# A stick-breaking and retention step: values and gates of one head as one 512-column row panel, in place of two-head value panels and gate panels

## The chip, the cores and the metric

The kernel runs on one core of a Trainium2 chip. The metric is the device time of one execution in microseconds. The kernel before takes 2279.3 us, the median of three runs (2276.02 to 2281.19).

A core has TensorE for matmuls (PE in the profile; its loads of the stationary operand are PEld), VectorE (DVE), ScalarE (ACT), GpSimd (POOL) and SyncE (SP), which here only issues transfers. Each engine works through its own list of instructions in order, and semaphores tie the lists together. ACT, POOL and SP each issue DMAs from their own list, so a transfer also waits for what stands ahead of it there.

## The reference

One layer of a hybrid encoder, for 1024 prompt frames and 8 x 16 sample frames (one tile of 128), with a model width of 2048 and 8 heads of 128 in each of two groups. One projection gives eight parts; stick-breaking attention and retention work on four each; each head's output is normalised and multiplied by the SiLU of its gate; then comes one output projection.

```python
p = jnp.einsum('btd,de->bte', rms_norm(x, norm_pre), w_in)
q_sb, k_sb, v_sb, gate_sb, q_r, k_r, v_r, gate_r = jnp.split(p, splits, axis=-1)
# stick-breaking
z = jnp.einsum('bqhd,bkhd->bhqk', q, k) * (HEAD_DIM ** -0.5)
later = lax.cumsum(log_keep, axis=3, reverse=True) - log_keep
a = jnp.where(strict, jnp.exp(log_beta + later), 0.0)
o_sb = jnp.einsum('bhqk,bkhd->bqhd', a, v)
# retention, by chunks, with a state s
o_r = intra(q, k) @ v + decay_read * (q @ s)
# merge
y = concat(head_rms_norm(o_sb, g_sb) * silu(gate_sb), head_rms_norm(o_r, g_r) * silu(gate_r))
x = x + rms_norm(y @ w_out, norm_post)
```

## The kernel before

**Tiles and groups.** The frames are nine tiles of 128. Group g0 is tiles 0 to 3 and the sample tile, 640 columns in pieces of 256 and 384; group g1 is tiles 4 to 7, 512 columns in one piece. Stage 2 goes through g0 and then g1, and in each through the eight heads.

**Products.** Every large product is split in three: a number is taken as a rounded part (hi) and a rest (lo), and hi x hi, hi x lo and lo x hi are summed. `split` (L167, L168) makes both parts: ACT copies the rounded part (wh), DVE subtracts it (wl). So each weight block of 256 KB needs a load (wr, on SP's queue, five buffers), an ACT pass and a DVE pass (four buffers) before PE can use it.

**Panels.** A column panel (`project`, L401; matmul L387) keeps the weights stationary and moves the tokens of a group: 16 blocks of 128 rows, three terms each. A head has six: retention's queries and keys (parts 4, 5) and gate (7), attention's queries and keys (0, 1) and gate (3). A row panel (`project_rows`, L424; matmul L446) keeps a tile of tokens stationary and moves 256 weight columns, the values of two heads; so one is computed for each part and each pair of heads. `gate` (L475) multiplies a gate panel by the root of the norm, takes its sigmoid on ACT and multiplies both.

**Order.** The side work of the heads (scores, scans, transposes, decode, retention) is written as jobs that yield a number of ticks. `tick` (L228) adds one to a clock and lets at most one job take a step; a panel ticks as it emits its products, 48 times for a column panel. Constants such as D_TO, D_TI (from a turn-out to its turn-in and on to its transpose) and D_VC (between the two sets of decode's value products) are counted in these ticks. `drain(job)` ticks until a job has ended, whether products are emitted or not. The scheduler then sets each engine's list by this order and its priorities.

**Side work that the change touches or moves.** `decode` (L796) computes the sample tile's scores against cached keys (zc, L822), then `pd` from cached values: eight loads vc (L849) into a ring of V_BUFS = 6 buffers that the cached keys kcT also use, in two sets of four (L886). `sample_retention` updates the samples' states (pSs, pa, L1011; ro). `Out.finish` (L705) normalises a head's output, sends it to DRAM (s_o, turn-out on ACT's queue), fetches it turned (so, ro, turn-in on SP's queue), transposes it (L716) and multiplies it by gain and gate. `stick_breaking` (L727) runs z (L753), sigmoids, scan (L682), product (L683), turn-out and turn-in (be), transpose (L743) and pa (L783). `retention` has rs (L913) and pa (L931).

**PSUM.** The tags acc0 and acc1 have two banks each. z has two more (score_tile).

**End of stage 2 and stage 3.** The output projection is computed as seven products (n = 1 to 7) of blocks; product(5) for g0 runs at the end of stage 2, then the remaining jobs are drained. Stage 3 (matmuls L1210, L1213, L1214; tokens stationary, 512 weight columns moving) starts with product 1 for both groups.

Of the kernel before, what the change touches and what calls it, by code (L numbers as in the profile page):

```python
# [18 lines left out]
P = 128  # L19
# [13 lines left out]
COLS = (0, 1, 3, 4, 5, 7)  # L33
ROWS = (2, 6)
# [54 lines left out]
def tile_hybrid_step(  # L89
# [138 lines left out]
    def tick():  # L228
        clock[0] += 1
        for job in jobs:  # L230
            if job.at <= clock[0]:
                wait = step(job)
                jobs.remove(job)
                if wait is None:
                    job.done = True
                else:
                    job.at = clock[0] + wait
                    jobs.append(job)
                return
# [184 lines left out]
    def project_rows(g, mov, col, dst, off, loads=None, roots_first=None):  # L424
        hi, lo = mov
        nt = len(g["tiles"])
        banks = [
            accp.tile([P, 2, 2 * P], F32, name=f"accn{b}", tag=f"acc{b % 2}") for b in range((nt + 1) // 2)
        ]
        for w in range(KT // 2):  # L430
            wr = wp.tile([P, 2, 2 * P], F32, name="wrn", tag="wr", bufs=5)
            nc.sync.dma_start(wr, w_rows[ROWS.index(col[0]), col[1] // 2, :, 2 * w : 2 * (w + 1), :])
            for _ in range(WQ // 2 if loads and w < 2 else 0):
                next(loads, None)
            wh = wp.tile([P, 2, 2 * P], F32R, name="whn", tag="wh")
            wl = wp.tile([P, 2, 2 * P], F32R, name="wln", tag="wl")
            split(wh, wl, wr)
            for j in range(2):
                q, jj = divmod(2 * w + j, WQ)
                for t in range(nt):  # L440
                    a = banks[t // 2][:, t % 2, :]
                    ts = slice(t * P, (t + 1) * P)
                    for n, (lhs, rhs) in enumerate(((hi, wh), (hi, wl), (lo, wh))):


                        anchor[0] = nc.tensor.matmul(  # L446
                            a,
                            lhs[q][:, jj, ts],
                            rhs[:, j, :],
                            start=(w == 0 and j == 0 and n == 0 and t % 2 == 0),  # L450
                            stop=(w == KT // 2 - 1 and j == 1 and n == 2 and (t % 2 == 1 or t == nt - 1)),
                        )
                    tick()
        if roots_first:
            roots_first()
        for t in range(nt):
            at = tiles_before(g) + t
            nc.scalar.activation(
                dst[:, off + t].rearrange("p j d -> p (j d)"), banks[t // 2][:, t % 2, :], AF.Copy,
                scale=root_of[:, at : at + 1],  # L460
            )

    with ExitStack() as s1:
# [11 lines left out]
        def gate(acc, tag):  # L475
            e = ep.tile([P, NMAX], F32, name=tag, tag=tag)
            for a, (o, m) in acc:
                rooted(e[:, o : o + m], a, o, m)
                s = ep.tile([P, 512], F32, name="sw", tag="sw", bufs=1)
                nc.scalar.activation(s[:, :m], e[:, o : o + m], AF.Sigmoid)  # L480
                nc.vector.tensor_tensor(e[:, o : o + m], e[:, o : o + m], s[:, :m], ALU.mult)
            return e
# [14 lines left out]
        pair = {}  # L497

        def ret_values(g, mov, h, loads=None, roots_first=None):
            pair["r"] = ep.tile([P, 5, 2, P], F32, name="rv", tag="rv")  # L500
            project_rows(g, mov, col(6, h), pair["r"], 0, loads, roots_first)

# [8 lines left out]
        with tc.tile_pool(name="p0", bufs=2) as p0, tc.tile_pool(name="p0s", bufs=1) as p0s, tc.tile_pool(  # L511
            name="p0p", bufs=4, space=PSUM
# [92 lines left out]
            ret_values(g0, mov, 0, None, roots_first)  # L605
# [3 lines left out]
            first = *first, pair["r"][:, :, 0, :], dict(rg=gate(project(g0, mov, col(7, 0)), "rg"))  # L609
# [15 lines left out]
        def store_rows(tiles, n, off, dst_p, dst_s, h):  # L625
            nc.scalar.dma_start(dst_p[h, :, tiles[0] : tiles[0] + 4, :], n[:, off : off + 4, :])
            if SAMPLE in tiles:
                nc.scalar.dma_start(dst_s[h], n[:, off + 4, :])

        par = const.tile([P, 2, 4, 2, DS], F32, name="par")  # L630
        nc.vector.memset(par, 0.0)
        for j in range(2):
            nc.vector.memset(par[:, j, :, j, :], 1.0)
        parf = par.rearrange("p a c j t -> p a (c j t)")
# [60 lines left out]
        class Out:  # L695
# [5 lines left out]
            def done(self, i):  # L701
                sq = op.tile([P, P], F32, name="sq", tag="sq")
                nc.scalar.activation(sq, self.o[:, i, :], AF.Square, accum_out=self.ssq[:, i : i + 1])

            def finish(self, b, h, gT, oT, dst):  # L705
                rs = inv_rms(op, self.ssq, P, "o")
                nc.vector.tensor_tensor(
                    self.o, self.o, rs.unsqueeze(2).to_broadcast([P, self.nt, P]), ALU.mult
                )
                s = turn_out(self.o, f"s_o{b}_{h}_{self.nt}_{phase[0]}")  # L710
# [6 lines left out]
                nc.vector.scalar_tensor_tensor(  # L717
                    gT[:, :n], oT[:, :n], gains[:, b, h : h + 1], gT[:, :n], ALU.mult, ALU.mult
                )
                nc.scalar.dma_start(dst, gT[:, : self.nt * P])  # L720
# [6 lines left out]
        def stick_breaking(g, h, out, q2, k2, rest):  # L727
            todo = [(i, t) for i, t in enumerate(g["tiles"]) if t != SAMPLE]
            lag, kinds = 2, ("psr" if todo[0][1] else ("kp", "be", "cp"))
            rows = []  # L730
            for step in range(len(todo) + lag):
# [39 lines left out]
                if step >= lag:  # L771
# [6 lines left out]
                    while "vn" not in rest:  # L778
                        yield 3
                    vn = rest["vn"]  # L780
                    po = acc_tile()
                    for j in range(t + 1):
                        nc.tensor.matmul(po[:, :P], at[:, j, :], vn[:, j, :], start=(j == 0), stop=(j == t))  # L783
# [12 lines left out]
        def decode(h, qs, rest):  # L796
            i = 4
            out = Out(1, "do")
            qp = op.tile([P, 2, P], F32, name="qp", tag="qp", bufs=1)
            nc.vector.tensor_tensor(  # L800
                qp, qs.unsqueeze(1).to_broadcast([P, 2, P]), parf, ALU.mult
            )
# [71 lines left out]
            while "vn" not in rest:  # L874
                yield 3
            vn = rest["vn"]
            po = psd.tile([P, 512], F32, name="pd", tag="pd")
            nc.tensor.matmul(po[:, 2 * P : 3 * P], at[:, 8, :], vn[:, i, :], start=True, stop=True)
# [21 lines left out]
            while "sg" not in rest:  # L900
                yield 3
            last_row = slice(4 * P, 5 * P)
            oT = op.tile([P, P], F32, name="doT", tag="doT", bufs=1)
            Job(out.finish(0, h, rest["sg"][:, last_row], oT, s_y[0][h][:, last_row]))
# [117 lines left out]
        def ret_branch(gi, g, h, rq, rk, rv, rest):  # L1022
# [15 lines left out]
            while "rg" not in rest:  # L1038
                yield 3
            yield from out.finish(1, h, rest["rg"], rk, s_y[gi][H + h])  # L1040

        def sb_branch(gi, g, h, out, q2, k2, kT, rest):
# [9 lines left out]
            store_rows(tiles, rest["vn"], off, v_prompt, v_sample, h)  # L1052
            if gi == 0:
                nc.scalar.dma_start(s_v[h], rest["vn"][:, :4, :])
            while "sg" not in rest:
                yield 3
            yield from out.finish(0, h, rest["sg"][:, :NB_TOK], kT, s_y[gi][h][:, :NB_TOK])
# [17 lines left out]
        ret_job = sb_job = sub = loads = after = None  # L1075
# [504 lines left out]
```

## Time and profile before

| what | us |
|---|---|
| median of three runs | 2279.3 |
| profiled execution, span | 2278.3 |
| column panels, matmul L387, all pieces and terms, busy | 1989.9 |
| row panels, matmul L446, busy | 979.6 |
| split of 128x512 weight blocks on ACT (L167), mean of one | 0.631 |
| split of 128x512 weight blocks on DVE (L168), mean of one | 0.689 |
| load of a weight block wr from issue to landing, median | 4.4 |
| turn-out s_o<-so, and turn-in so<-s_o, median | 4.2, 3.0 |

A matmul's busy time in the groups overlaps that of its neighbours (the two sums above are longer than the span), so the pitch of matmuls is read from unbroken runs in the chain, not from the mean of one. In a row of the chain the columns are start, length and what ran, with the number of instructions joined. In the waits, a row names an engine and line, what it waited for, the total, the number of times and the longest. In the groups, a row gives line, engine, operation, tiles and shapes, count, then busy time and mean nanoseconds of one, then idle time ahead of it and its cause.

### The profile page before, as it was taken

To read this page: it belongs to the slowest core of one execution; us is meant where nothing else is said; L and a number is where in the kernel's file an instruction comes from. 1 tells how busy PE (TensorE), PEld (TensorE's weight loads), DVE (VectorE), ACT (ScalarE), POOL (GpSimd) and SP (SyncE) were. 2 spreads that over 40 slices of the span, in tenths; PEclk is the share of its full clock that TensorE was granted. 3 is DMA by queue.
4 is the path that set the end of the run, shared out by engine and by line. 5 is a ranking of instruction groups with operands and counts; after the bars stand their busy time and mean duration, and the time that the engine had idled before them with its cause. 6 is when DMAs were issued, how large, how long until landed. Compare 5 with 4: busy or idle time off the path is not lost.

```text
span 2278.3 us, 38962 instructions
## 1 busy us (share of the span) xinstructions
PE 2241.5 (98%) x14306; PEld 2023.3 (89%) x14306; DVE 1263.7 (55%) x2606; ACT 919.8 (40%) x1951; POOL 340.6 (15%) x577
## 2 busy tenths in 40 slices
PE   8999999999999999999999999999999999999998
PEld 8999999999999999999887989888888988788886
DVE  5435544454545454456556665766665667555567
ACT  6433333333333333335343334343343445435363
POOL 0012120301202030121111111120212212000020
PEclk9999999999999999999999999999999999999999
DMA  8747656675656657578778888878787758865596
GB/s 284 233 153 199 196 159 194 176 220 159 182 194 181 194 165 209 177 200 269 193 225 207 220 220 235 206 226 238 220 231 213 216 165 190 252 205 182 146 222 172
DMA packets 440832, 463.13 MB, mean 203 GB/s; under 512 B 182336, under 2 KB 302144, under 8 KB 440128
## 3 DMA queue, kind: packets, MB, share of 16 engines
q1 hardware_dynamic: 318400, 300.16, 46.5%
q0 software_dynamic: 28720, 78.41, 12.3%
q10 hardware_dynamic: 93520, 82.07, 11.4%
q8 instruction: 112, 1.84, 0.3%
q14 instruction: 80, 0.66, 0.1%
HBM read 359.58 MB, written 110.36 MB: 206 GB/s over the span
## 4 chain that ended last, share of the span: by engine, by line
PE 88%; DMA 5%; DVE 3%; issue 2%; ACT 2%; SPq 0%; POOL 0%; DVEq 0%; ACTq 0%; POOLq 0%
PE acc L387 46%; PE accn L446 17%; PE a L1213 5%; PE a L1214 5%; PE a L1210 5%; PE pa L783 3%; PE z L753 2%; PE pd L886 1%; PE zc L822 1%; DMA ro<-s_rk 1%; DMA s_rk<-rk 1%; PE pa L931 1%; PE pS L946 1%; DVE kp L682 1%; DMA wr<-w_cols 1%
## 5 line engine op out<-in xcount | busy, mean ns | idle before, releaser
L387 PE MATMUL acc<-mh,wh 128*128 128x256 f32 (+2 forms) x2304 | 667.4, 341 | 6.9 <-ACT wh L167 6.9
L387 PE MATMUL acc<-ml,wh 128*128 128x256 f32 (+2 forms) x2304 | 662.7, 340 | 0.2
L387 PE MATMUL acc<-mh,wl 128*128 128x256 f32 (+2 forms) x2304 | 659.8, 338 | 0.0
L168 DVE TENSOR_TENSOR wl<-wr,wh 128x512 fp32r<-128x512 f32 x504 | 345.9, 689 | 428.0 <-ACT wh L167 401.7
L167 ACT ACTIVATE wh<-wr 128x512 fp32r<-128x512 f32 x504 | 317.3, 631 | 641.2 <-PE acc L387 347.2
L387 PEld LDWEIGHTS acc<-mh,wh 128*128 128x128 f32 x2304 | 421.4, 189 | 39.2 <-ACT wh L167 6.9
L387 PEld LDWEIGHTS acc<-ml,wh 128*128 128x128 f32 x2304 | 422.9, 189 | 32.1 <-issue 3.3
L387 PEld LDWEIGHTS acc<-mh,wl 128*128 128x128 f32 x2304 | 425.5, 189 | 27.8 <-DVE wl L168 0.2
L446 PE MATMUL accn<-whn,mh 128*128 128x256 f32 x1152 | 328.1, 285 | 0.0
L446 PE MATMUL accn<-wln,mh 128*128 128x256 f32 x1152 | 325.8, 283 | 0.8 <-DVE wln L168 0.8
L446 PE MATMUL accn<-whn,ml 128*128 128x256 f32 x1152 | 325.7, 283 | 0.0
L446 PEld LDWEIGHTS accn<-whn,mh 128*128 128x128 f32 x1152 | 220.7, 192 | 2.7 <-issue 0.8
L446 PEld LDWEIGHTS accn<-wln,mh 128*128 128x128 f32 x1152 | 220.7, 192 | 1.8 <-DVE wln L168 1.0
L446 PEld LDWEIGHTS accn<-whn,ml 128*128 128x128 f32 x1152 | 220.7, 192 | 0.0
L167 ACT ACTIVATE whn<-wrn 128x512 fp32r<-128x512 f32 x128 | 80.5, 632 | 183.2 <-PE acc L387 74.2
L168 DVE TENSOR_TENSOR wln<-wrn,whn 128x512 fp32r<-128x512 f32 x128 | 87.6, 687 | 117.4 <-ACT whn L167 113.5
L646 POOL DMA_DIRECT2D be<-s_be x128 | 94.1, 741 | 149.5 <-DMA s_be<-be 126.4
L682 DVE TENSOR_TENSOR_SCAN kp<-kp 128x1152 f32<-128x1152 f32 (+4 forms) x40 | 82.7, 2067 | 45.7 <-POOL kp L671 29.1
L809 POOL DMA_DIRECT2D kcT<-cache_k x64 | 34.6, 545 | 442.2 <-PE pd L886 268.2
L1210 PE MATMUL a<-wh,mh 128*128 128x512 f32 x240 | 94.0, 392 | 1.8 <-ACT wh L167 1.8
L671 POOL TENSOR_SCALAR_AFFINE_SELECT kb<-kb 128x128 f32<-128x128 f32 x64 | 29.8, 474 | 433.2 <-ACT kb L665 430.9
L1213 PE MATMUL a<-wl,mh 128*128 128x512 f32 x240 | 94.3, 393 | 0.2 <-DVE wl L168 0.2
(272 smaller groups left out, 2968.7 us busy)
## 6 DMA issues: line engine op xcount, KB each, us to landing
wr<-w_cols SPq DMA_DIRECT2D x384, 256.0 KB, 4.4
wrn<-w_rows SPq DMA_DIRECT2D x128, 256.0 KB, 3.7
kcT<-cache_k POOLq DMA_DIRECT2D x64, 512.0 KB, 8.2
vc<-cache_v SPq DMA_DIRECT2D x64, 512.0 KB, 6.0
wr<-s_b SPq DMA_DIRECT2D x80, 256.0 KB, 4.1
br<-w_out SPq DMA_DIRECT2D x64, 256.0 KB, 4.9
s_b<-br ACTq DMA_DIRECT2D x32, 512.0 KB, 5.5
wr<-w_out SPq DMA_DIRECT2D x48, 256.0 KB, 3.7
```

The costliest lines, as they stand in the source:

```text
L167: nc.scalar.activation(hi, src, AF.Copy),
L168: nc.vector.tensor_tensor(lo, src, hi.bitcast(F32), ALU.subtract),
L387: last = nc.tensor.matmul(a[:, :m], lhs[:, j, :], rhs[w][:, j, o : o + m], start=(w == 0 and j == 0 and n == 0), stop=(w == KT // WQ - 1 a ...
L446: anchor[0] = nc.tensor.matmul(a, lhs[q][:, jj, ts], rhs[:, j, :], start=(w == 0 and j == 0 and n == 0 and t % 2 == 0), stop=(w == KT // 2 ...
L646: q.dma_start(raw[32 * i : 32 * i + 32, :].rearrange("p (k a) -> p k a", a=32), s[:, :, 32 * i : 32 * i + 32].rearrange("k (j b) a -> b (k ...
L682: nc.vector.tensor_tensor_scan(rev, rev, rev, 1.0, ALU.mult, ALU.bypass)
L753: nc.tensor.matmul(z[:, :c], q2[a][:, i * P : (i + 1) * P], k2[b][:, s : s + c], start=(m == 0), stop=(m == 2),)
L783: nc.tensor.matmul(po[:, :P], at[:, j, :], vn[:, j, :], start=(j == 0), stop=(j == t))
L809: ready.append((kc, nc.gpsimd.dma_start(kc, cache_k[h, m // 4, m % 4])))
L1210: ins = nc.tensor.matmul(a, hi[k][:, ts], wh, start=first, stop=False)
L1213: nc.tensor.matmul(a, hi[k][:, ts], wl, start=False, stop=False)
L1214: anchor[0] = nc.tensor.matmul(a, lo[k][:, ts], wh, start=False, stop=last)
```

## The change

The values and gates of one head become one row panel of 512 columns (v_sb, v_ret, g_sb, g_ret). The two gate panels of a head and the row panels of two heads go. The panel of five tiles needs five PSUM banks: four are acc0 and acc1 twice, the fifth in g0 is a z bank (in head 0 one of another pool). Each tile's bank is read by ACT (copy of 256 columns, sigmoid of 256) and DVE (256). The gate is then in rows and not in columns, so `finish` multiplies by it ahead of the turn-out, and only the gain comes after the transpose.

```diff
-    def project_rows(g, mov, col, dst, off, loads=None, roots_first=None):
+    def project_rows(g, mov, part, extra, out, loads=None, ready=None):
...
+        banks = [accp.tile([P, 512], F32, name=f"accm{t}", tag=f"acc{t % 2}") for t in range(4)]
+        if nt > 4:
+            banks.append(extra())
+        for k in range(KT):
...
+            for t in range(nt):
+                ts = slice(t * P, (t + 1) * P)
+                for n, (lhs, rhs) in enumerate(((hi, wh), (hi, wl), (lo, wh))):
+                    anchor[0] = nc.tensor.matmul(
+                        banks[t],
...
+                    if n:
+                        tick(0.75)
...
+            def out(t, a, root):
+                vt, ut = (x[:, t].rearrange("p j d -> p (j d)") for x in (v, u))
+                nc.scalar.activation(vt, a[:, : 2 * P], AF.Copy, scale=root)
+                nc.scalar.activation(ut, a[:, 2 * P :], AF.Sigmoid, scale=root)
+                nc.vector.scalar_tensor_tensor(ut, a[:, 2 * P :], root, ut, ALU.mult, ALU.mult)
+
+            project_rows(g, mov, w_rows[h], extra or (lambda: score_tile("accm4")), out, loads, ready)
...
-                nc.vector.tensor_tensor(
-                    self.o, self.o, rs.unsqueeze(2).to_broadcast([P, self.nt, P]), ALU.mult
-                )
+                for i in range(self.nt):
+                    nc.vector.scalar_tensor_tensor(
+                        self.o[:, i, :], self.o[:, i, :], rs[:, i : i + 1], gated[gi, h][:, at + i, b, :], ALU.mult, ALU.mult
+                    )
...
+                nc.vector.tensor_scalar(flat, oT[:, :n], gains[:, b, h : h + 1], None, ALU.mult)
```

The order of a head's panels changes, and with it where the jobs fall. The last head of g1 computes retention's queries and keys as one pair, with the loads of the first output products between. Product 1 for g0 moves into stage 2, ahead of the drains, and stage 3 begins with product 1 for g1 alone; the weights of n = 1 are loaded and split for each.

```diff
+                def ret_both():
+                    rest = first_left()
+                    accs = project_pair(g, mov, (col(4, h), col(5, h)), rest)
+                    for _ in rest:
+                        pass
+                    ret_finish(accs[0])
+                    ret_keys(accs[1])
+
+                def ret_finish(acc):
                     drain(ret_job)
                     rows_in["rq"] = rope(acc, "rq", *ropes)
...
-                    order = ret_queries, ret_keys, ret_gate, attention, gates
-                elif h == H - 3:
-                    order = ret_queries, ret_keys, attention, ret_gate, gates
+                    order = rows, ret_queries, ret_keys, attention
                 elif h == H - 2:
-                    order = ret_queries, attention, ret_keys, ret_gate, gates
+                    order = rows, ret_queries, attention, ret_keys
                 else:
-                    order = attention, ret_queries, ret_keys, ret_gate, gates
+                    order = rows, attention, ret_both
...
         drain(nxt)
+        for nh in range(2):
+            Job(collect(1, nh, product(1, nh, (0,), True, D_OUT)), 1)
         drain(ret_job)
         drain(sb_job)
...
-        for n, groups in ((1, BOTH), (2, BOTH), (5, G1), (3, BOTH), (6, BOTH), (7, BOTH)):
+        for n, groups in ((1, G1), (2, BOTH), (5, G1), (3, BOTH), (6, BOTH), (7, BOTH)):
```

The pacing constants keep their values. Smaller edits: the sample queries' mask is replaced by two copies into a tile that is zeroed once, and the values of g0's frames are loaded into a tile of their own for g1.

**The first place: decode's values on PE, in g0.** Before, in the head whose decode is pd_5472, the second set of four cached-value products stands 74 rows of PE behind the first, with products of the panel on both sides (vc is a cached-value block, acc0 and acc1 the panel's banks):

```order
L886 MATMUL pd_5472<-vc_5339,kp_4329 32x256 x4
L886 MATMUL pd_5472<-vc_5389,kp_4329 32x256 x4
L886 MATMUL pd_5472<-vc_5516,kp_4329 32x256 x4
L886 MATMUL pd_5472<-vc_5518,kp_4329 32x256 x4
L387 MATMUL acc0_5621<-ml1_179,wh_5659 128x256
L387 MATMUL acc1_5622<-ml1_179,wh_5659 128x384
```

Now, in the same head (pd_4798), both sets stand together, and right behind them the first product with a new weight block:

```order
L859 MATMUL pd_4798<-vv_2704,kp_3846 128x128
L867 MATMUL pd_4798<-vc_4606,kp_3846 32x256 x4
L867 MATMUL pd_4798<-vc_4608,kp_3846 32x256 x4
L867 MATMUL pd_4798<-vc_4714,kp_3846 32x256 x4
L867 MATMUL pd_4798<-vc_4730,kp_3846 32x256 x4
L867 MATMUL pd_4798<-vc_4741,kp_3846 32x256 x4
L867 MATMUL pd_4798<-vc_4747,kp_3846 32x256 x4
L867 MATMUL pd_4798<-vc_4844,kp_3846 32x256 x4
L867 MATMUL pd_4798<-vc_4846,kp_3846 32x256 x4
L386 MATMUL acc0_4958<-mh3_182,wh_5096 128x256
L386 MATMUL acc1_4959<-mh3_182,wh_5096 128x384
```

vc_4844 and vc_4846 use the buffers of vc_4606 and vc_4608, so their loads stand behind the first two of these rows; the products that lay between the sets have moved elsewhere.

**The second place: ACT behind the same decode.** Before, the decode's output do_4325 is squared, its root taken behind a table load, and then the split of a later block, wh_5888, follows; the turn-out s_o comes after it:

```order
L167 ACTIVATE wh_5826<-wr_5824 128x512
L703 ACTIVATE sq_5702,ssq2_4326<-do_4325 128x128
L183 ACT_TABLE_LOAD
L183 ACTIVATE or_5708<-ov_5707 128x1
L167 ACTIVATE wh_5888<-wr_5886 128x512
L639 DMA s_o0_2_1_0_5718<-do_4325 128x128
```

Now the turn-out of do_3842 stands ahead of the split as well, and the split is that of wh_5096, which the row of PE right behind pd uses:

```order
L628 DMA s_rk0_3_4989<-rk_4945 128x5x128
L692 ACTIVATE sq_5038,ssq2_3843<-do_3842 128x128
L182 ACTIVATE or_5044<-ov_5043 128x1
L628 DMA s_o0_2_1_0_5054<-do_3842 128x128
L166 ACTIVATE wh_5096<-wr_5094 128x512
```

No split of the panel stands between two steps of that chain any more, and the table load is gone.

**The third place: DVE at the end of stage 2.** Before, in the last head of g1, splits of weight blocks (wl) stand between the passes on the keys (kT, kl), the scan of a row (kp, be) and the rope of the retention queries (rq):

```order
L716 STREAM_TRANSPOSE kT_19397<-so_19312 128x512
L717 SCALAR_TENSOR_TENSOR sg_20147<-kT_19397,gains_77,sg_20147 128x512
L168 TENSOR_TENSOR wl_20489<-wr_20486,wh_20488 128x512
L468 TENSOR_TENSOR kT_20354<-acc0_20264,roots_79 128x512
L168 TENSOR_TENSOR wl_20532<-wr_20529,wh_20531 128x512
L168 TENSOR_TENSOR kl_20356<-kT_20354,kh_20355 128x512
L168 TENSOR_TENSOR wl_20550<-wr_20547,wh_20549 128x512
L682 SCALAR_TENSOR_TENSOR kp_20399<-kp_20399 128x640
L683 TENSOR_TENSOR be_20400<-be_20400,kp_20399 128x640
```

Now the rope of rq comes first, then the keys, additions of output weights (br) and three scans, with no split of a panel's block from here on until the pair is done:

```order
L167 TENSOR_TENSOR wl_18585<-wr_18582,wh_18584 128x512
L488 TENSOR_TENSOR sw_18629<-sw_18629,sinT_10625 128x512
L489 TENSOR_TENSOR rq_18628<-acc0_18210,cosT_10624 128x512
L490 TENSOR_TENSOR rq_18628<-rq_18628,sw_18629 128x512
L706 STREAM_TRANSPOSE kT_17338<-so_17252 128x512
L303 TENSOR_TENSOR br_18102<-br_18102 128x256
L707 TENSOR_SCALAR so_17252<-kT_17338,gains_77 128x512
L303 TENSOR_TENSOR br_18102<-br_18102 128x256
L461 TENSOR_TENSOR kT_18200<-acc0_18066,roots_79 128x512
L303 TENSOR_TENSOR br_18223<-br_18223 128x256 x4
L167 TENSOR_TENSOR kl_18202<-kT_18200,kh_18201 128x512
L671 SCALAR_TENSOR_TENSOR kp_18254<-kp_18254 128x640
```

The keys' panel is held in its bank until kT_18200 is made, and z of this head needs kl_18202; both now stand behind rq, whose panel ends later than the keys' own.

227 lines of the change are left out of this document (84 added, 143 removed).

## The prediction

> **What bounds the kernel now.** I read the page's busy times first, then the chain that ended last, then the waits of TensorE (PE).
>
> ```profile
> PE 2241.5 (98%) x14306; PEld 2023.3 (89%) x14306; DVE 1263.7 (55%) x2606; ACT 919.8 (40%) x1951; POOL 340.6 (15%) x577
> PE 88%; DMA 5%; DVE 3%; issue 2%; ACT 2%; SPq 0%; POOL 0%; DVEq 0%; ACTq 0%; POOLq 0%
> ```
>
> PE is busy 98% of 2278.3 us and makes up 88% of the chain. DVE has 45% of the span free, so what it does costs only where a matmul stands behind it. The kernel is a queue of matmuls, and the time is their pitch plus the holes. The waits of PE (engine, line, what was waited for: total us, times, longest) give the holes:
>
> ```profile
> PE pa L783 <- DVE kp L743: 8.1, 7, 2.4
> PE acc L387 <- ACT wh L167: 6.9, 1, 6.9
> PE pb L557 <- DVE dg L555: 3.1, 1, 3.1
> PE a L1210 <- ACT wh L167: 1.8, 1, 1.8
> PE pS L946 <- DVE rkn L1036: 1.5, 2, 1.0
> ```
>
> All thirteen rows of that view come to 25.8 us. The 6.9 is the first load, so 18.9 us of holes lie inside the program. Two things can therefore change the time: the pitch of the matmuls, and how well the order on PE covers the work of the others.
>
> **The matmuls that the change replaces.** The chain shows unbroken runs (start, us, what, count), which give clean pitches, and the groups give the counts:
>
> ```profile
> 121.17 3.24 PE accn L446 x27
> 174.96 2.65 PE acc L387 x18
> 1146.02 12.73 PE acc L387 x56
> 1939.89 0.23 PE a L1213
> ```
>
> ```profile
> L446 PE MATMUL accn<-whn,mh 128*128 128x256 f32 x1152 | 328.1, 285 | 0.0
> L387 PE MATMUL acc<-mh,wh 128*128 128x512 f32 x768 | 302.4, 394 | 0.0
> L387 PE MATMUL acc<-mh,wh 128*128 128x384 f32 x768 | 260.5, 339 | 0.0
> L387 PE MATMUL acc<-mh,wh 128*128 128x256 f32 x768 | 222.5, 290 | 6.9 <-ACT wh L167 6.9
> ```
>
> A 256-column row matmul costs 3.24/27 = 0.120 us. The 256 and 384 pieces of the columns panels average 2.65/18 = 0.1472, and a 512 piece costs 12.73/56 = 0.2273. Tokens stationary with 512 weight columns moving is what stage 3 does already, at 0.23. Each group stands for one of three terms, so there are 3 x 1152 = 3456 row matmuls. The gates are two of six column panels, a third of each group: 3 x 256 = 768 matmuls of each size.
>
> Removed: 3456 x 0.120 + 1536 x 0.1472 + 768 x 0.2273 = 414.7 + 226.1 + 174.6 = 815.4 us. Added: 8 heads x 16 blocks x 9 tiles x 3 = 3456 matmuls of 512, x 0.2273 = 785.5. **The term is -30 us**: the columns are the same, and 2304 matmuls fewer save 13 ns each.
>
> [...]
>
> **What stands off the path.** Evacuating the panel takes the same two ACT passes and one DVE pass per tile. Gate multiplications move ahead of the turn-out; DVE's total hardly changes. Sigmoids beside the values save ACT table loads. The weights of n=1 are loaded and split once more, 16 blocks. All of this lies under products with DVE at 55% and ACT at 40%: nothing on the path as far as the order keeps splits ahead.
>
> Moving product (1, G0) ahead of the drains fills the hole at the start of stage 3: the 1.8 us of `a L1210` above, and its after-effect in the clock (next fence).
>
> **Holes cost the clock too.** Windows (busy of PE, PEld, DVE, ACT, POOL, then granted clock, DMA share, GB/s), and the timeline and chain at the stage boundary:
>
> ```profile
> 1235.00:1245.00 10.00, 7.56 (x39) 6.04 (x38) 5.57 (x10) 2.52 (x4) 0.00 (x0) 1.00 0.95 250
> 1245.00:1255.00 10.00, 10.00 (x56) 9.17 (x55) 5.89 (x23) 4.05 (x12) 0.00 (x0) 0.83 0.39 118
> ```
>
> ```profile
> 1964.59 0.49 PE L1210 MATMUL a<-wh,mh 128*128 128x512 f32 x1 [1.80 <-ACT wh L167]
> 1966.53 0.43 PE a L1210
> ```
>
> After 2.44 us of idling within ten, the clock was granted at 0.83 for the next ten: 1.7 us lost. After the 1.80 us hole eight matmuls ran at 0.43 instead of 0.23, 1.7 us again. So the old boundary cost 1.8 + 1.7 = **3.5 us, which goes**; and each new hole of some length costs 1.7 more.
>
> [...]
>
> **What the change takes from the cover.** The pacing numbers (D_VC, D_TO, D_TI) stay, but a head has fewer ticks: g0 6 x 48 + 80 = 368 before, 4 x 48 + 120 = 312 after (80 and 120 are the row panel's; before, half of two heads' pairs). `drain(ret_job)` in ret_finish then runs the missing ticks without products. I see three places in the order.
>
> (a) *Decode's values, g0.* There are six buffers for eight loads, so the seventh and eighth load wait for the first two pd groups. Before, 74 product rows lay between the two sets of pd; after, all eight stand together.
>
> ```profile
> L849 SPq DMA_DIRECT2D vc<-cache_v x64: 327/372/1469, 142.3 to 1132.9; - x64
> DMA to landing us min/median/max: 3.7/6.0/11.0
> 214.32 1.86 PE pd L886 x32
> 227.24 1.86 PE pd L886 x32
> ```
>
> One set is four loads in 1.86 us, 0.465 a load; now 227.24 - 214.32 - 1.86 = 11.1 us cover the reload. After, five groups cover it: 2.3 us. The load takes 6.0 (3.7 to 11.0), so PE waits 3.7 us (1.4 to 8.7) a head. Seven heads have it (the eighth's sets stay apart), two of them with 13 products (1.9) more to cover it: 5 x 3.7 + 2 x 1.8 = **22 us**. A queue of SP stands behind these loads, the next weight block's load among it; it lands while pd waits.
>
> (b) *The split behind decode's finish.* ACT holds wh_5096 of the next block behind sq, or and the turn-out of `do`, which need pd's end; PE needs it right after pd. Before, the same chain ran under products, in the timeline:
>
> ```profile
> 492.59 0.29 DVE L894 COPY do<-pd 128x128 f32<-128x128 f32 x1 [2.00 <-PE pd L886]
> 492.92 0.74 DVE L896 SCALAR_TENSOR_TENSOR do<-pd,dec,do 128x128 f32<-128x128 f32 x2
> 493.69 0.31 ACT L703 ACTIVATE sq<-do 128x128 f32<-128x128 f32 x1 [3.83 <-DVE do L896]
> 493.91 0.19 ACT L703 ACTIVATION_READ_ACCUMULATOR sq<-do 128x1 f32 x1
> 494.12 0.15 DVE L182 TENSOR_SCALAR ov<-ssq 128x1 f32<-128x1 f32 x1 [0.47 <-ACT sq L703]
> 495.40 0.20 ACT L183 ACTIVATE or<-ov 128x1 f32<-128x1 f32 x1
> 495.51 0.61 ACT L167 ACTIVATE wh<-wr 128x512 fp32r<-128x512 f32 x1
> 496.16 0.69 DVE L168 TENSOR_TENSOR wl<-wr,wh 128x512 fp32r<-128x512 f32 x1
> ```
>
> From 492.59 to wh's end, 496.12, is 3.5 us, with a table load of 1.28 in it. After, that load goes (no sigmoid in between), and instead the root's four small steps (0.15 each), one 128-column product (0.35) and the issue of the turn-out come in ahead of wh: again about 3.5 us, of which nothing is covered. Bounds: 0 if ACT reached wh first, which its order excludes, so 2.5 to 4.5. Seven heads: **24 us**, after (a), since pd's end is its start.
>
> (c) *The samples' state update, g0.* pa waits for `ro`, which stands on DVE behind the decode row's scan, behind sigmoids of zc and zn:
>
> ```profile
> L682 DVE TENSOR_TENSOR_SCAN kp<-kp 128x1152 f32<-128x1152 f32 x8 | 21.1, 2636 | 16.6 <-POOL kp L677 9.9 <-ACT wh L167 6.7
> L666 ACT ACTIVATE be<-zc 128x512 f32<-128x512 f32 x16 | 9.5, 593 | 0.0
> L682 DVE TENSOR_TENSOR_SCAN kp<-kp 128x768 f32<-128x768 f32 x8 | 14.5, 1816 | 10.5 <-POOL kp L671 10.5
> L683 DVE TENSOR_TENSOR be<-be,kp 128x768 f32<-128x768 f32 x8 | 7.5, 942 | 0.4
> L304 DVE TENSOR_TENSOR br<-br 128x256 f32<-128x256 f32 x192 | 80.5, 419 | 4.1 <-DMA br<-s_y 2.5
> ```
>
> Two sigmoids 1.2, two more and a copy of 128 columns at 0.3 (as sq above), the scan 2.64 and the two `ro` 0.7 (as the two of `do`): 5.4 us. Between zc and pa PE has 14 products (2.1) and seven small matmuls, about 3.4. Six heads at 2.0: **12 us** (0 to 20).
>
> (d) *End of stage 2.* Behind the last panel pair, DVE's queue holds from sw_18629 to the transpose of kp_18254: scans and products of rows of 640, 768 and 896 columns, 3 x (1.82 + 0.94) = 8.3; 14 additions at 0.42, 5.9; 14 passes over 512 columns (rope, four splits for stage 3, kT, the finish) at 0.69 as wl above, 9.7; eight small ones at 0.29, 2.3; the transpose 0.8: 27 us, without a split of the panel between. PE has 48 products of rk (10.9), 18 of z (7296 columns, 3.3) and a few small ones ahead of pa_18354: 14.6. **12 us** (6 to 16).
>
> (e) *From g0 to g1*, where three drains of 36, 39 and 27 ticks run and the first row panel's loads stand behind turn-outs:
>
> ```profile
> s_b<-br ACTq DMA_DIRECT2D x32, 512.0 KB, 5.5
> wrn<-w_rows SPq DMA_DIRECT2D x128, 256.0 KB, 3.7
> ```
>
> One of each in a row is 9.2 us; with a block of three products each for four or five tiles in hand, between 0 and 8 of it shows. I take **4**.
>
> Together 22 + 24 + 12 + 12 + 4 = 74 us. A wait gives time to those behind it. The same reckoning on the kernel before gives 22.6 us where the view of waits shows 18.9, a share of 0.84: **+62 us**. The clock adds 1.7 at seven decode ends and two boundaries: **+15** (0 to 25, the upper if the 2 us holes count).
>
> Sum on the profiled span: 2278.3 - 30 - 3.5 + 62 + 15 = 2321.8. The median shown is 1.0 above that span: **2323 us, 2% slower**.
>
> **Rivals.**
> - *The pitch wins.* Place: decode's end in g0, (a) and (b). They decide: with (c), (d) and (e) at 28 x 0.84 = 24 us, the break-even of 33.5 leaves 9.5 us for seven heads, 1.4 a head. That needs loads at their 3.7 minimum and (b) hidden. DMA at 5% of the chain speaks for it; the order of ACT against. With (a) at 1.4 for five heads, (b) nothing, the rest halved and no clock loss: 2279.3 - 33.5 + 7 + 12 = about 2265.
> - *No difference*: (b) is hidden after all (-20), the clock loses half (-8), and (d) and (e) find their cover (-13): 2323 - 41 = 2282.
> - *Reload at its slow end*: loads of 8 to 11 us when pd's two reloads meet the turn-ins and weight loads on SP's queue. At 9 us (a) grows by 3 x 7 = 21, and clock by 10: about 2354.
> [...]
>
> **Chances.** Forecast 0.55, slow reload 0.17, pitch not given 0.06, pitch wins 0.16, no difference 0.06. A difference of 0.2% (4.6 us) is about what a measurement of this kernel can tell from none. Faster 0.17, same 0.05, slower 0.78. The range goes from 2268, which leaves out the better half of the pitch case, to 2360, above the slow reload's centre.
>
> **What would show it.** In the profile after: unbroken runs of the row panel at 0.227 (the -30); waits of PE `pd L867` for DMA vc, near 3.7 us, seven times; `acc L386 <- ACT wh` some 3.5 us right behind; `pa L989 <- DVE ro` near 2; a wait of `pa L768` or `rs L891` near the end of stage 2 of 6 us or more; granted clock below 1 after them. If the waits of PE stay below 40 us in all, the forecast is wrong. It is also wrong if SP's queue shows the reloads issued early, that is, if a pd group frees its buffer long before.

## The result, and the profile after

The changed kernel takes **2446.5 us**, the median of four runs (2444.22 to 2451.56), against 2278.8 for the kernel before on the same chip (2276.02 to 2281.19). The ratio is 1.074, with an interval of 1.072 to 1.076. The forecast was 2323 us, with a range up to 2360: the sign was right, the size was wrong by more than a factor of three. The profiled execution has a span of 2442.5 us, 164 more than before.

The busy times and the shares of the chain that ended last, on the page of the changed kernel:

```profile
PE 2258.3 (92%) x12002; PEld 1914.5 (78%) x12002; DVE 1270.7 (52%) x2708; ACT 899.5 (37%) x1967; POOL 364.7 (15%) x577
PE 78%; DMA 9%; issue 4%; DVE 4%; ACT 2%; POOL 1%; SPq 1%; ACTq 0%; DVEq 0%; POOLq 0%
```

PE has the 2304 matmuls fewer that the change promises (14306 to 12002). Yet it is busy 16.8 us longer, and the rest of the span, in which it is idle, grows from 2278.3 - 2241.5 = 36.8 to 184.2 us. So the 164 us are 147 of new holes and 17 of longer matmuls. DMA rises from 5% to 9% of the chain, although its work has hardly changed (467.03 MB for 463.13): transfers have moved onto the path.

The waits of PE in the changed kernel, without its smaller rows (total us, times, longest):

```profile
PE acc L386 <- ACT wh L166: 83.7, 9, 13.8
PE pd L867 <- DMA vc<-cache_v: 21.1, 11, 4.7
PE pa L989 <- DVE ro L974: 14.3, 6, 2.7
PE rs L891 <- DVE rk L490: 6.5, 1, 6.5
PE pa L768 <- DVE kp L731: 6.0, 4, 3.4
PE pa L768 <- DVE kb L731: 5.7, 5, 3.4
PE a L1175 <- ACT wh L166: 5.2, 1, 5.2
PE rs L891 <- DVE sc L893: 4.9, 1, 4.9
PE accm L441 <- DVE kT L461: 4.2, 2, 2.8
PE accm L441 <- DVE wln L167: 3.8, 2, 3.4
PE a L1175 <- ACT ah L166: 3.8, 1, 3.8
PE acc L386 <- DVE rq L489: 3.1, 1, 3.1
PE a L1178 <- DVE wl L167: 2.9, 2, 2.1
```

One row holds half of it. The first load is 7.65 of its 83.7; the other 76 us are seven holes of 8.6 to 13.8 us and a small one, a long one in each of the first seven heads of g0, right behind the decode's value products. The forecast had this very place, at 24 us.

**One such hole, row by row.** It ends at 559.62. The timeline around it (start, us, engine, line, operation; in brackets the idle time before and its releaser):

```profile
526.57 1.27 SPq L833 DMA_DIRECT2D vc<-cache_v  x2
534.58 0.33 SPq L635 DMA_DIRECT2D so<-s_o  x1
543.68 0.81 SPq L833 DMA_DIRECT2D vc<-cache_v  x2
544.53 1.50 SPq L635 DMA_DIRECT2D so<-s_o  x3
546.12 7.85 SPq L375 DMA_DIRECT2D wr<-w_cols  x5
549.07 1.08 PE L867 MATMUL pd<-vc,kp 128*32 128x256 f32 x8 [0.99 <-DMA vc<-cache_v]
558.94 2.73 ACT L166 ACTIVATE wh<-wr 128x512 fp32r<-128x512 f32 x4 [6.80 <-DMA s_o<-do]
```

Between 527.8 and 543.7 SP issues one small turn-in and nothing else. From 534.9 on the seventh value load stands at the head of its queue; it waits for a buffer that the first pd group frees (at 543). Behind it stand three turn-ins and then the next five weight loads, which leave only from 546.12 on. The landing of these five loads, from the tile view of wr, and the transfers of 543 to 559 (number, KB each, median us to landing):

```profile
DMA to landing us min/median/max: 9.5/10.7/12.8
```

```profile
kcT<-cache_k POOLq DMA_DIRECT2D x6, 512.0 KB, 7.6
wr<-w_cols SPq DMA_DIRECT2D x5, 256.0 KB, 10.7
vc<-cache_v SPq DMA_DIRECT2D x2, 512.0 KB, 4.3
```

Each landing took 9.5 to 12.8 us, where the median over the program is 3.5. The first load left at 546.1, and 12.8 us later is 558.9, when ACT starts on wh. (The releaser in ACT's row, s_o, is inferred from what ended last before it; wh reads only its own weight block. In other heads the same row names the load itself: at 710.67 and 1008.20 ACT's wh had waited 7.98 and 7.42 us for DMA wr.) Windows of the stretch ahead, the hole and what follows (length, busy of PE, PEld, DVE, ACT, POOL, then granted clock, DMA share, GB/s) show what the loads met:

```profile
536.00:543.70 7.70, 7.70 (x66) 7.32 (x68) 2.88 (x4) 0.87 (x2) 0.00 (x0) 1.00 0.27 86
543.70:559.00 15.30, 3.79 (x56) 1.35 (x48) 2.30 (x11) 0.66 (x4) 3.23 (x6) 0.65 0.98 329
559.60:565.00 5.40, 5.38 (x20) 5.38 (x21) 3.58 (x6) 1.89 (x3) 0.00 (x0) 0.50 0.89 267
565.00:565.50 0.50, 0.50 (x4) 0.50 (x3) 0.00 (x0) 0.00 (x0) 0.00 (x0) 0.65 1.16 200
565.50:566.00 0.50, 0.50 (x6) 0.50 (x5) 0.15 (x1) 0.21 (x1) 0.00 (x0) 1.00 1.09 168
```

While SP's queue was held up, the DMA engines were busy at 0.27 and PE worked through the weights it had. Then the pd groups freed the ring, and six kcT loads, two vc loads and five weight loads came at once: 0.98 of the DMA engines for 15 us, with PE working a quarter of that time. When the products resumed, the clock was granted at 0.50 until about 565.35 (from the mean of 0.65 in the half microsecond from 565.0) and at 1.00 from then on: 5.7 us at half clock, which cost 2.9 us on top of the hole.

### The profile page after: what moved, and what is told of

It is laid out like the page before. It is cut to its first block, busy times and chain, and to the rows that moved or that the text cites. A ratio compares the mean times of both kernels' runs of the same rounds, so it can differ in the third digit from the quotient of the medians.

```text
span 2442.5 us, 34608 instructions
## 1 busy us (share of the span) xinstructions
PE 2258.3 (92%) x12002; PEld 1914.5 (78%) x12002; DVE 1270.7 (52%) x2708; ACT 899.5 (37%) x1967; POOL 364.7 (15%) x577
## 2 busy tenths in 40 slices
DMA packets 440047, 467.03 MB, mean 191 GB/s; under 512 B 182592, under 2 KB 298304, under 8 KB 439360
## 4 chain that ended last, share of the span: by engine, by line
PE 78%; DMA 9%; issue 4%; DVE 4%; ACT 2%; POOL 1%; SPq 1%; ACTq 0%; DVEq 0%; POOLq 0%
PE accm L441 31%; PE acc L386 26%; PE a L1178 4%; PE a L1175 4%; PE a L1179 4%; DMA wr<-w_cols 3%; PE pa L768 2%; PE z L741 2%; DMA so<-s_o 1%; DVE kp L671 1%; PE zc L806 1%; PE pd L867 1%; PE pa L909 1%; PE pS L924 1%; PE rs L891 1%
## 5 line engine op out<-in xcount | busy, mean ns | idle before, releaser
L386 PE MATMUL acc<-mh,wh 128*128 128x256 f32 (+2 forms) x1536 | 456.3, 348 | 86.8 <-ACT wh L166 83.7
L441 PE MATMUL accm<-whn,mh 128*128 128x512 f32 x1152 | 449.9, 395 | 7.6 <-DVE kT L461 4.2
L441 PE MATMUL accm<-wln,mh 128*128 128x512 f32 x1152 | 451.5, 392 | 4.0 <-DVE wln L167 3.8
L386 PE MATMUL acc<-ml,wh 128*128 128x256 f32 (+2 forms) x1536 | 453.5, 346 | 0.0
L386 PE MATMUL acc<-mh,wl 128*128 128x256 f32 (+2 forms) x1536 | 452.2, 345 | 0.7 <-DVE wl L167 0.7
L441 PE MATMUL accm<-whn,ml 128*128 128x512 f32 x1152 | 452.8, 393 | 0.0
L167 DVE TENSOR_TENSOR wl<-wr,wh 128x512 fp32r<-128x512 f32 x392 | 268.4, 688 | 307.9 <-ACT wh L166 304.6
L386 PEld LDWEIGHTS acc<-mh,wl 128*128 128x128 f32 x1536 | 291.2, 194 | 22.1 <-DVE wl L167 1.8
L441 PEld LDWEIGHTS accm<-whn,mh 128*128 128x128 f32 x1152 | 216.6, 189 | 52.6 <-DVE kT L461 5.5
L441 PEld LDWEIGHTS accm<-whn,ml 128*128 128x128 f32 x1152 | 217.2, 189 | 50.6 <-issue 5.9
L441 PEld LDWEIGHTS accm<-wln,mh 128*128 128x128 f32 x1152 | 217.5, 189 | 49.7 <-DVE wln L167 6.0
L1178 PE MATMUL a<-wl,mh 128*128 128x512 f32 x240 | 94.7, 395 | 2.1 <-DVE wl L167 2.1
```

The costliest lines, as they stand in the source:

```text
L167: nc.vector.tensor_tensor(lo, src, hi.bitcast(F32), ALU.subtract),
L386: last = nc.tensor.matmul(a[:, :m], lhs[:, j, :], rhs[w][:, j, o : o + m], start=(w == 0 and j == 0 and n == 0), stop=(w == KT // WQ - 1 a ...
L441: anchor[0] = nc.tensor.matmul(banks[t], lhs[q][:, j, ts], rhs, start=(k == 0 and n == 0), stop=(k == KT - 1 and n == 2),)
L1178: nc.tensor.matmul(a, hi[k][:, ts], wl, start=False, stop=False)
```

## The experiments

All ratios are to the kernel before, run beside each kernel on the same chip. Except for the fifth, each edit is to the changed kernel. First the three that ask where the 76 us come from.

**1. The two late value loads of a head on POOL's queue**, so that nothing of SP stands behind them. The wait for a buffer stays.

```diff
-                ld = nc.sync.dma_start(vc, cache_v[h, k])
+                ld = (nc.sync if k < V_BUFS else nc.gpsimd).dma_start(vc, cache_v[h, k])
```

> Only the queue of decode's two late value loads changes: they go on GpSimd's queue in place of SyncE's. Theory A (the weight loads stand on SyncE behind a load that waits for pd, and then come down in one burst): the weight loads go out some 15 us earlier in a head, the waits of acc L386 for ACT wh fall from 83.7 us to 35 or less (the first load's 7.7 and seven times the 3.5 us of the chain from pd to the turn-out of do, which ACT still holds ahead of wh), the waits of pd for vc stay near 21, and the time falls by 45 to 75 us, to 2370 to 2400. Rival B (the weight loads are late because six key loads take the DMA engines at the same moment): the key loads still go out at pd, so the wait stays above 60 and the time within 15 us of the changed kernel's 2446. Rival C (the split is late because of ACT's own order, as predicted): nothing changes.

Measured: 2401.9 us, ratio 1.054 [1.051, 1.056], so 45 us less than the changed kernel, just above the range of theory A. Its waits, and SP's rows of the timeline in the same head:

```profile
PE pd L867 <- DMA vc<-cache_v: 33.6, 13, 6.1
PE acc L386 <- ACT wh L166: 31.4, 9, 7.4
```

```profile
515.86 1.11 SPq L833 DMA_DIRECT2D vc<-cache_v  x2
527.04 6.98 SPq L375 DMA_DIRECT2D wr<-w_cols  x5
```

From the fifth and sixth value load to the first weight load it is 11.2 us here and 19.6 in the changed kernel (526.57 to 546.12): the weight loads leave 8.4 us earlier. The view of who waited for these loads gives ACT's wh 47.6 us in the changed kernel and 3.8 here:

```profile
ACT wh L166: 47.6, 14
```

```profile
ACT wh L166: 3.8, 1
```

The key loads still leave behind the first pd groups (from 534.39 on, on POOL's queue), so their transfers alone, rival B, don't make the hole.

What is left for PE behind wh is 31.4 - 7.4 for the first load = 24.0 us, the total that the forecast had for the chain of decode's finish on ACT. The match is partly luck: it is 4.3 to 4.6 us in three heads, in which the turn-out stands ahead of the split as in the changed kernel, and 2.6 in four, in which ACT's list now has the split first. At 4.4 in all seven the chain would be some 31 us, an estimate from these rows. So between 45 and 52 us of the 76 were the loads in SP's queue. PE's idle time falls by 46 us (to 2401.5 - 2263.2 = 138.3) rather than the 52 by which its waits for wh fell, because pd now waits longer for its reloads: 33.6 for 21.1.

**2. The row panel's pace.** `tick(0.75)` for two of its three products makes 120 ticks of a g0 head's panel, so a head has 312. Counted as the program is built, `drain(ret_job)` runs 60 more in most g0 heads without a product, so the jobs ask for 372. A pace of 1.125 makes the panel's 120 into 180, and the head's 312 into 372.

```diff
-                        tick(0.75)
+                        tick(1.125)
```

> Only the row panel's tick goes from 0.75 to 1.125, so that a head of the first group has 372 ticks as before the change and its drains without products fall from 60 to 6 ticks. Theory D (the holes come from ticks that pass without products): decode's two sets of values part again, the waits of acc L386 for ACT wh fall under 30 us, those of pd for vc under 15, and the time falls to 2320 to 2370. Rival E (the holes come from the order of the panels, which stays): waits of acc for wh above 60, time above 2420.

Measured: 2407.5 us, 1.056 [1.054, 1.058]. The waits, then the landing of the five weight loads at the decode of the same head, from their tile view:

```profile
PE acc L386 <- ACT wh L166: 57.1, 8, 8.7
PE acc L386 <- DVE gg L478: 21.0, 6, 4.1
PE pd L867 <- DMA vc<-cache_v: 4.4, 4, 2.1
```

```profile
DMA to landing us min/median/max: 3.7/4.1/14.5
```

The time lies between the two expectations. Almost no tick of g0 is left to run empty (six a head), and the wait for the reloads is nearly gone from PE, since 19 products now run between the parts of pd. But the holes behind wh stay at some 8 us in six heads (the first has none now), and in six heads there is a new hole of 3 to 4 us (gg, the gate's evacuation). SP's queue still has the weight loads behind the reloads (issued from 526.3 and from 523.8), and the slowest, the first one, lands 14.5 us after its issue; ACT's wh starts then. In the whole run ACT's wh waits 43.7 us for such loads, against 47.6. So what is left behind wh is lost by the weight loads, not by the reloads.

**3. The same, to 1.5**, which makes the panel's ticks 240 and a g0 head's 432.

```diff
-                        tick(0.75)
+                        tick(1.5)
```

> Row panel's tick 1.5: no drain is left in the heads of either group, nor in the last pair's 214 ticks. Theory D: waits of acc for wh under 15 us, of pd for vc under 6, the hole at the end of stage 2 (15 us of rs and pa now) half as large, time 2260 to 2300, so at or below the kernel before: then the 30 us of the matmuls show. Rival E: above 2420. Rival F (jobs stepped twice as densely in the row panel crowd DVE there): the waits of accm L441 for DVE or ACT, 11 us now, grow above 30, time 2310 to 2350.

Measured: 2288.3 us, 1.0047 [1.0032, 1.0061]. That is inside theory D's range, but not at or below the kernel before. Of the 168 us that the change lost, 158 are back. The busy times, and five of the largest waits (the rows of pa L768, 7.0 us in two, are left out):

```profile
PE 2228.9 (98%) x12002; PEld 1885.4 (83%) x12002; DVE 1261.1 (55%) x2708; ACT 918.0 (40%) x1981; POOL 346.1 (15%) x577
```

```profile
PE acc L386 <- ACT wh L166: 8.4, 2, 7.5
PE a L1175 <- ACT wh L166: 4.6, 1, 4.6
PE a L1175 <- ACT ah L166: 4.3, 1, 4.3
PE a L1178 <- DVE wl L167: 3.8, 3, 1.9
PE a L1175 <- ACT kp L654: 2.5, 1, 2.5
```

All of (a), (b), (c) and most of (d) are gone, though the panel, its gates and the loads are as in the change. The trace shows what moved: the 64 pd matmuls of a head, from 542.98 on in the changed kernel, have no product between them there; with a pace of 1.5 they are two blocks of 32 with 76 products between; before, it was 74.

**4. Is it the missing ticks, or the larger pace itself?** Here the pace stays at 0.75, and the jobs ask for fewer ticks, so that `drain(ret_job)` in ret_finish has nothing left to run in g0.

```diff
-D_ZC = 24
-D_ROW = 18
-D_VC = (6, 46)
+D_ZC = 16
+D_ROW = 12
+D_VC = (6, 36)
...
-D_TO = (32, 23)
+D_TO = (12, 23)
...
-D_TI = (32, 13)
+D_TI = (12, 13)
```

> The changed kernel with its tick of 0.75 and only the first group's pacing numbers shortened (turn-out to turn-in 12 for 32, turn-in to transpose 12 for 32, key sets 16 for 24, decode row 12 for 18, value sets 36 for 46), so that no tick is drained at a head's retention queries in the first group. Theory D (drained ticks): the holes of the first group go, waits of acc L386 for ACT wh from 83.7 to under 25, of pa L989 for ro to under 4, time 2320 to 2350, the second group's and the end of stage 2's holes stay. Rival: the numbers were the transfers' real time, and turn-ins now stand in the queues before their data, time above 2400. Rival F (more ticks in the row panel is what helped, by spreading the work): above 2400 too.

Measured: 2322.0 us, 1.019 [1.017, 1.021], 124 us less than the changed kernel and within theory D's range:

```profile
PE acc L386 <- ACT wh L166: 15.0, 4, 7.3
PE pa L768 <- DVE kb L731: 10.2, 6, 2.5
PE rs L891 <- DVE rk L490: 6.5, 1, 6.5
PE rs L891 <- DVE sc L893: 5.0, 1, 5.0
PE pd L867 <- DMA vc<-cache_v: 3.3, 2, 2.2
PE acc L386 <- DVE rq L489: 3.1, 1, 3.1
```

With `drain(ret_job)` empty in g0, most of the holes of decode go (7.3 of the 15.0 is the first load), by another edit than in the run before. The smaller holes of pa behind kb grow, from 5.7 to 10.2. In g1 the jobs still run dry (245 ticks in its eight heads, and 214 ahead of the last pair), and the end of stage 2 keeps its holes within a tenth: rk 6.5, sc 5.0, rq 3.1.

**5. The joined sets alone, in the kernel before.** The second set of cached values is due one tick behind the first.

```diff
-D_VC = (6, 46)
+D_VC = (6, 1)
```

> The kernel before, with the second set of decode's value products 1 tick behind the first in place of 46; nothing else. The sets then stand within about 20 products of each other and the reloads show as in the changed kernel, but in SyncE's queue they stand behind the next weight blocks' loads and not ahead of them. Theory A (the queue's order makes the large part): waits of pd for vc 12 to 20 us, waits of acc for wh small, time 2295 to 2315. Rival: joined sets alone make the holes, with the key loads' burst at pd: waits of acc for wh above 40 us, time 2340 or more.

Measured: 2286.9 us, 1.004 [1.003, 1.005], so 9 us, less than either expectation. The profiled execution is the fastest of the eight (2281.0), so its rows show why there is no large hole, but not where the 9 us are. PE's only wait at that place, SP's rows of one decode, and the transfers of its next 16 us:

```profile
PE pd L886 <- DMA vc<-cache_v: 2.3, 6, 0.7
```

```profile
463.35 1.26 SPq L376 DMA_DIRECT2D wr<-w_cols  x2
476.97 0.80 SPq L849 DMA_DIRECT2D vc<-cache_v  x2
477.87 6.43 SPq L376 DMA_DIRECT2D wr<-w_cols  x4
```

```profile
kcT<-cache_k POOLq DMA_DIRECT2D x6, 512.0 KB, 11.6
wr<-w_cols SPq DMA_DIRECT2D x4, 256.0 KB, 8.2
```

This run is close to the second experiment: 48 pd matmuls together, then 11 products, 8, 8 products and 8. SP's queue is held up here too (464.6 to 476.97), four weight loads go behind the reloads, and they land late (8.2 us at the median, 10.7 in the changed kernel). Yet there is no hole. The difference in the rows is that two weight loads went out ahead of the hold-up, at 463.35, so that ACT has blocks to split and PE products to run while the burst lands. So neither joined sets nor the burst costs much by itself in that kernel. That they cost 76 us where PE reaches decode's end with no weights in hand is read from these rows; no run varied the weights in hand alone.

**6. The moved product.** Product (1, G0) goes back from the end of stage 2 into stage 3, with the old pace, with a pace of 1.5 and with one of 1.35.

```diff
-        for nh in range(2):
-            Job(collect(1, nh, product(1, nh, (0,), True, D_OUT)), 1)
...
-        for n, groups in ((1, G1), (2, BOTH), (5, G1), (3, BOTH), (6, BOTH), (7, BOTH)):
+        for n, groups in ((1, BOTH), (2, BOTH), (5, G1), (3, BOTH), (6, BOTH), (7, BOTH)):
```

> Undoes one part: product 1 of the first group goes back from the end of stage 2 to the start of stage 3, with its weights loaded once. If that part gives what was predicted (the old hole at the start of stage 3 filled, 3.5 us), the time rises by 2 to 8 us. Rival: the moved product only stands among drains that leave holes anyway, and the time stays within 3 us; or it makes the two holes of 3.8 and 5.2 us that stage 3 now has, and the time falls by 5 to 12.

> The changed kernel with the row panel's tick at 1.5 and product 1 of the first group back in stage 3. Undoing the moved product gave 7.4 us with the old tick. If the two add, 2288.3 falls by 5 to 10, to 2278 to 2283, and the waits of a L1175 for ACT wh and ah (8.9 us in the run with tick 1.5) fall under 3. Rival: the moved product filled the boundary once the drains are gone, as predicted, and the time rises by 2 to 6.

> As before, with tick 1.35: no drain is left in the first group, 33 ticks in the second. If only drained ticks count, the time is within 5 us of tick 1.5, a little above it. If the density of steps in the row panel costs something of its own, the time lies below tick 1.5 by 3 to 8.

Measured: with the old pace 2439.1 us, 1.070 [1.068, 1.072]; with 1.5, 2289.2 us, 1.0053 [1.0040, 1.0065]; with 1.35, 2303.4 us, 1.011 [1.010, 1.013]. So moving the product lost some 7 us with the old pace, with intervals that barely part (its upper end is 1.0722, the lower end of the changed kernel 1.0723), and is worth nothing with 1.5 (2289.2 and 2288.3 with overlapping intervals). The two edits do not add. In the profile with the old pace the place has other holes: 7.0 us of a L1175 that the profile calls issue, and 5.0 of rs L891 behind a load. The pace of 1.35 is 14 us slower than 1.5, though no drain runs dry in g0 with either; neither expectation had that, and it is not explained.

**7. What is left of the difference with a pace of 1.5.** Three kernels, all with it: the reloads on POOL's queue as in the first experiment, and two with shorter counts, D_TO = (32, 14) and D_TI = (32, 8), then D_TO = (24, 18) and D_TI = (24, 10).

> Ticks of 1.5 in the row panel, and the two late value loads on POOL's queue. If the row panel's larger tick has already put products between the sets of pd, SP's queue is not blocked any more, and the second edit is worth nothing: 2284 to 2292 us, as with the tick alone. If part of the queue's block is left in the clock or in small waits, it gains 3 to 8 us: 2280 to 2285.

> Ticks of 1.5, and turn-in to transpose cut from 23 to 14 ticks and from 13 to 8, so that the last heads' jobs have fewer ticks to run without products at the end of stage 2. Theory: the 10 us that are left over the kernel before are holes at that end (some 11 us in the profile of the run with the tick alone) and their clock; then 2276 to 2285. Rival: the left-over is the clock and small waits all over stage 2, and shorter waits bring transposes too early: 2287 to 2300.

> As the run before, with the turn-out's count cut too (32 to 24) and less cut from the second numbers (18 and 10). Same theory: 2276 to 2286; rival: 2287 to 2300.

Measured: 2290.4 us, 1.0061 [1.0036, 1.0085]; 2293.9, 1.0070 [1.0054, 1.0086]; 2297.7, 1.0086 [1.0069, 1.0103]. The queue edit, worth 45 us at the old pace, is worth nothing here, as it would be if both edits cure the same loss. Both kernels with shorter counts came out in their rivals' range: the holes of stage 3 stayed (ah 3.9, wh 4.7 in the second kernel), so the theory that shorter counts bring the rest fell. No version beat the kernel before; the nearest is the pace of 1.5 alone.

## Why the forecast was wrong, point by point

| term | forecast, us | by the rows after |
|---|---|---|
| fewer matmuls | -30 | -27 |
| hole at the start of stage 3 and its clock | -3.5 | about +10 of idle time |
| (a) reloads of vc | 22 | 21.1 |
| (b) wh behind decode's finish | 24 | 76, of it 24 to 31 the chain itself |
| (c) samples' state update | 12 | 14.3 |
| (d) end of stage 2 | 12 | 17.9 |
| (e) g0 to g1 | 4 | 1.9, and 7.5 in the next panel |
| slower matmuls behind holes | +15 | +40 |

**The matmuls: right.** A run of the chain without a break, in the kernel with the pace of 1.5, gives the row panel's pitch:

```profile
44.46 50.13 PE accm L441 x220
```

It is 0.228 a matmul, x 3456 = 788 us, for the 815.4 of the products replaced: -27. The forecast's 13 ns for each of the 2304 matmuls came out as 12, and the change does what it says.

**(a) and (c): right**, in place and size. For (a) the total fits better than the heads: six of the seven wait, for 2.2 to 6.4 us, and the first does not.

**(b) is the step that failed.** The forecast said: "A queue of SP stands behind these loads, the next weight block's load among it; it lands while pd waits." It had seen the queue, and then priced what stands in it at nothing. The runs showed in its place: not one but five blocks stood there, held back 8 us; PE used up the weights in hand meanwhile; and the five came down together with 4 MB of cached keys and values, so that a landing took 9.5 to 12.8 us and ended 9 us behind pd. The first experiment splits the term: 24 to 31 us of ACT's chain, and 45 to 52 of the loads.

**The clock was mis-sized**: 15 us forecast as nine holes at 1.7. PE is busy 16.8 us longer where 27 less was due, so its matmuls lost about 44 us. The granted clock gives most of that. In windows of half a microsecond over the whole program, PE's busy time multiplied by what the clock falls short of 1 adds up to 5.0 us before, 45.2 after and 7.8 with a pace of 1.5. So the clock took 40 us more than before. Of the 45.2, 18 lie around the seven long holes (16 of them behind), 8 behind shorter holes of g0, and 18 from g1 on. The runs that closed the holes got it back: at a pace of 1.5 PE's busy time is 29.4 us shorter than after, and the mean granted clock 0.995 for 0.961. Behind each of the seven long holes it stood at 0.50 and came back to 1.00 at 3.6 to 6.2 us behind the first product, 5.7 in the one shown above. That cost 16 / 7 = 2.3 us a hole, so the forecast's price of 1.7, read behind holes of 1.80 and 2.44 us, was too low for them.

**The moved product has the wrong sign.** The old hole of 1.8 us did go, but stage 3 has three rows in its place, ah 3.8, wh 5.2 and wl 2.9: 11.9 for 2.0 before. The sixth group of runs puts the move at a loss of some 7 at the old pace.

**(d) and (e) were under-sized**: 6.5 + 4.9 + 3.1 + 3.4 (the longest of kp) = 17.9 at the end of stage 2; a hole of 3.4 behind kb in the first head was not forecast; and the first panels of g1 lose 2.8 (kT), 1.3 and 3.4 (row weights) that the forecast did not have. The factor of 0.84 on all holes had no ground in the new order.

**Above the single terms**, the forecast counted 368 and 312 ticks a head and saw the drain, but priced only the ends of what falls into it. One number of the pace brings back 158 of the 168 us, another set of counts 124. How many ticks run empty doesn't give the time by itself: with six left a head the second experiment still lost 129 us. By the rows of these runs, what decides is whether weights are in hand when decode ends.

**Of the rivals**, that of a slow reload was nearest in place, but it slowed the vc loads, which were not slow (5.1 median for 6.0); the slow ones were the weight loads behind them.

**What stays open.** With the pace of 1.5 the kernel should gain the 27 us and is 10 slower. PE idles 55.0 us for 36.8, 18 more, of which 13 are the four rows at L1175 and L1178 (15.2, for 2.0 before); and it is busy 12.6 less instead of 27, so some 14 us more of busy time than the new pitch gives. The clock accounts for 2.8 of them (7.8 for 5.0). No run here closed those holes, and it wasn't shown where the other 11 or 12 us are.

## What to carry to other kernels

When a change takes products out of a loop that also paces the side work, count what the side work asks for and what the loop now gives before pricing anything else: here fitting g0's jobs to the fewer ticks brought back 124 us in the fourth experiment, more than four times what the cheaper matmuls gained. When a load waits for a buffer, list what its queue holds behind it, price that as a burst when the queue opens (here five weight loads took 9.5 to 12.8 us to land, for 3.5 at the median over the program), together with the other queues that wait for the same event, and ask what is in hand until it has landed. Price a hole by holes like it: here the clock took 1.7 us behind holes of 1.80 and 2.44 us, and 2.3 in the mean behind the seven of 8.6 to 13.8.

## What the runs showed of the hardware that was not expected

A 256 KB weight load that lands in 3.5 us at the median took up to 12.8 us among 5 MB of others, at 329 GB/s and a DMA share of 0.98, right after a stretch at 86 GB/s. And the granted clock stood at 0.50 behind each of the seven long holes until 3.6 to 6.2 us behind the first product, in no order of the holes' length: 6.2 behind the hole of 13.8 (262.2 to about 268.4), 3.9 behind the one of 11.7, 3.6 behind the one of 10.1, 5.7 behind the one of 9.48. Behind the one of 1.80 in the kernel before it was still 1.00 for 0.6 us, and then 0.50 until 4.0 us behind the first product. As far as windows of a quarter of a microsecond show, it came back from 0.50 to 1.00 in one step each time.
